# Two of four weight sums formed by adding transfers instead of VectorE in the seven-product pairs of a decoder layer

## The chip, the cores and the metric

The kernel runs on one core of a Trainium2 chip. Its time is the device time of one execution in microseconds (us). Tensors stand in SBUF as 128 partitions by so many columns. TensorE (PE in the profile, PEld for its weight loads) multiplies, VectorE (DVE), ScalarE (ACT) and GpSimd (POOL) work element by element, and SyncE (SP) issues transfers between HBM and SBUF. POOL and ACT can issue transfers too.

## The reference

One decoder layer for 512 tokens of width 1024 in float32:

```python
h = rms_norm(x, ffn1_pre_g);  x = x + 0.5 * rms_norm(swiglu(h, ffn1_w_in, ffn1_w_out), ffn1_post_g)
h = rms_norm(x, mix_pre_g);   proj = h @ w_mix_in          # attention and a state space model
...
h = rms_norm(x, ffn2_pre_g);  x = x + 0.5 * rms_norm(swiglu(h, ffn2_w_in, ffn2_w_out), ffn2_post_g)

def swiglu(x, w_in, w_out):
    gate, up = jnp.split(x @ w_in, 2, axis=-1)             # w_in: 1024 x 5632
    return (jax.nn.silu(gate) * up) @ w_out                # w_out: 2816 x 1024
```

The change touches `x @ w_in` of the two feed-forward layers.

## The kernel before

Every float32 product is formed from two halves of its operands: `hi` (rounded by ScalarE, `whi`) and `lo` (the rest, `wlo = raw - hi`, by VectorE or POOL), and three matmuls hi·hi, hi·lo, lo·hi. Making `whi` and `wlo` of a weight tile is called a split (line 107 for `wlo`, 105 for `whi`); `cut` does it for a pair's tile, and there are four `whi`/`wlo` buffers, so a split of one product's weights waits for PE to have finished the product four before.

The 2816 hidden units are 22 blocks of 128. The first 8 (first layer) or 6 (second layer) are computed directly. The others come in pairs of blocks, f and f+1, by a scheme of Strassen's kind: the weights of a pair are a 2 x 2 array of tiles of 128 x 1024 floats (512 KB), a11 and a12 for the gate (first and second half of the inner dimension), a21 and a22 for the up projection. Seven products instead of eight need four sums of tiles: c3 = a11 + a21, c2 = c3 + a22, c1 = a21 + a22, and at last c2 + a12. On PE the products of a pair stand in this order, 24 matmuls of 256 columns each: `wx` with a11, `wy` with a12, `wx` with c2, `wq` with c1, `wx` with c3, `wq` with c2 + a12, `wx` with a22. In the chain of the profile two neighbouring `wx` products show as one piece of 48: a22 of one pair and a11 of the next. There are 7 pairs in the first layer (f = 8 to 20) and 8 in the second (f = 6 to 20); `outp`, the second matrix product (`yo`), stands between groups of them.

The function `seven` makes two closures: `sums` prepares sums and differences of the activations ahead of the pairs (n1, n2, t3, t4, in buffers `wsum`), and `pair` does one pair. a11 and a12 are loaded into buffers `wraw` (three, shared by all weights), a21 and a22 into `wx` (three), and all loads are issued by SP, in one order. VectorE forms the sums into `wsum` (three buffers) and makes `wlo`, except for a12 and a22, whose `wlo` is made by POOL (`cut(..., True)`). A scheduler sets the order on each engine by its own costs; only instructions marked `fix` keep the written order. Each engine works through its own list in order, so an instruction that waits holds up those behind it.

Of the kernel before, what the change touches and what calls it, by code (L numbers as in the profile page):

```python
# [8 lines left out]
F32 = mybir.dt.float32  # L9
# [3 lines left out]
ALU = mybir.AluOpType  # L13
# [4 lines left out]
P = 128  # L18
S = 512
# [3 lines left out]
NF = FF // P  # L23
# [3 lines left out]
QOFF = (0, 128, 384, 768, 1280)  # L27
RING = 8
NSTD = (8, 6)
PLACES = [(f"tq{q}{i}", 1) for q in range(3) for i in range(2)] + 3 * [("wsum", 3)]  # L30
BLOCKS = (2, 3, 0, 1)
HT = S // 2
H = 8
# [10 lines left out]
class Layer:  # L44
# [449 lines left out]
    def seven(self, fin, w_in, ig, r, ah, al):  # L494

        nc, V = self.nc, self.nc.vector
        more = [fin]  # L500
        wsum = lambda: more[0].tile([P, 1024], F32, name="wsum", tag="wsum", bufs=3)
        wx = lambda: fin.tile([P, 1024], F32, name="wx", tag="wx", bufs=3)
        gp = lambda: fin.tile([P, 1024], F32, name="gp", tag="gp", bufs=2)
        tq = []
        v4 = lambda t: t.rearrange("p (k c) -> p k c", c=HT)
        blocks = []

        def sums(early=False):

            q = [[gp(), gp()], [wx(), wx()]]  # L510

            def scaled(i):
                for j in range(2):
                    c = slice(j * HT, (j + 1) * HT)
                    for k in range(4):
                        V.scalar_tensor_tensor(out=v4(q[i][j])[:, k], in0=self.x(4 * i + k)[:, c],
                                               scalar=self.g(ig, 4 * i + k), in1=r[:, c], op0=ALU.mult, op1=ALU.mult)
                return q[i]

            b11, b12 = scaled(0)  # L520
            b21, b22 = scaled(1)
            more[0] = (yield) or fin
            tq.extend([more[0].tile([P, 1024], F32R, name="tq", tag=f"tq{i}{j}") for j in range(2)] for i in range(3))
            n1, n2, t4 = wsum(), wsum(), wsum()
            V.tensor_tensor(out=n1, in0=b11, in1=b12, op=ALU.subtract)
            yield
            bh, bl = [self.b16(n, F32R) for n in ("bh", "bl")] if early else (None, None)
            v = lambda t, i: t.rearrange("p (q k) c -> p q (k c)", q=4)[:, i]

            def plain(*ts):  # L530
                for t in ts:
                    i = len(blocks)
                    blocks.append((v(bh, i), v(bl, i)))
                    self.split(*blocks[i], t)

            if early:
                plain(b11)
            V.scalar_tensor_tensor(out=n2, in0=n1, scalar=-1.0, in1=b22, op0=ALU.mult, op1=ALU.subtract)
            if early:
                plain(b21)  # L540
            yield
            V.scalar_tensor_tensor(out=t4, in0=n2, scalar=-1.0, in1=b21, op0=ALU.mult, op1=ALU.subtract)
            self.split(*tq[0], n2)
            t3 = wsum()
            V.tensor_tensor(out=t3, in0=b22, in1=b12, op=ALU.subtract)
            yield
            if early:
                plain(b22, n1)
            yield
            self.split(*tq[1], t3)  # L550
            yield
            self.split(*tq[2], t4)
            if not early:
                yield
                bh, bl = [self.b16(n, F32R) for n in ("bh", "bl")]
                plain(b11, b21, b22, n1)
            yield

        def block(f, up, kh):
            t = wx() if up else self.wp.tile([P, 1024], F32, name="wraw", tag="wraw", bufs=3)  # L560
            src = w_in[f + NF * up:f + NF * up + 2, :, kh * S:(kh + 1) * S].rearrange("f p c -> p f c")
            nc.sync.dma_start(out=t.rearrange("p (f c) -> p f c", f=2), in_=src)
            return t

        def cut(t, pool=False):
            hi, lo = (self.wp.tile([P, 1024], F32R, name=n, tag=n, bufs=4) for n in ("whi", "wlo"))
            self.wsplit(t, hi, lo, pool)
            return hi, lo

        def times(bank, w, xb, first):  # L570
            for g in range(2):
                for k in range(4):
                    c, m = slice(k * HT, (k + 1) * HT), slice((4 * g + k) * P, (4 * g + k + 1) * P)
                    st = first and g == 0 and k == 0
                    for i, (wi, xi) in enumerate(((0, 0), (0, 1), (1, 0))):
                        self.mm(bank[:, g * HT:(g + 1) * HT], lhsT=w[wi][:, m], rhs=xb[xi][:, c],
                                start=st and i == 0, stop=g == 1 and k == 3 and i == 2, skip_group_check=True)

        def keep(bank):
            t = self.tmp("kp")  # L580
            nc.scalar.copy(out=t, in_=bank)
            return t

        def pair(f, late=False):
            (b11, b21, b22, n1), (n2, t3, t4) = blocks, tq
            add = lambda x, z, t: V.tensor_tensor(out=t, in0=x, in1=z, op=ALU.add)
            p2 = lambda t: t.rearrange("p (f c) -> p f c", f=2)
            half = lambda t, h: t[:, :, h * HT:(h + 1) * HT]
            gt = p2(gp())
            X = self.bank("wx")  # L590
            a11 = block(f, 0, 0)
            times(X, cut(a11), b11, True)
            s1 = keep(X)
            a12 = block(f, 0, 1)
            h12 = cut(a12, True)
            Y = self.bank("wy")
            times(Y, h12, b21, True)
            V.tensor_tensor(out=half(gt, 0), in0=p2(Y), in1=p2(s1), op=ALU.add)
            a21, a22 = block(f, 1, 0), block(f, 1, 1)
            c3 = wsum()  # L600
            add(a11, a21, c3)
            c2 = wsum()
            add(c3, a22, c2)
            times(X, cut(c2), n2, False)
            s2 = keep(X)
            c1 = wsum()
            add(a21, a22, c1)
            Q = self.bank("wq")
            times(Q, cut(c1), n1, True)
            q = keep(Q)  # L610
            times(X, cut(c3), t3, False)
            V.tensor_tensor(out=q, in0=X, in1=q, op=ALU.add)
            add(c2, a12, c2)
            times(Q, cut(c2), b22, False)
            V.tensor_tensor(out=half(gt, 1), in0=p2(Q), in1=p2(s2), op=ALU.add)
            nc.scalar.activation(out=gt, in_=gt, func=AF.Silu)
            times(X, cut(a22, True), t4, False)
            s = f % RING
            dst = lambda t, h: half(t.pair(slice(s, s + 2)), h)
            for h, u in ((1, q), (0, X)):  # L620
                V.scalar_tensor_tensor(out=half(gt, h), in0=p2(u), scalar=-1.0, in1=half(gt, h), op0=ALU.mult, op1=ALU.mult)
                if late:
                    self.split(dst(ah, h), dst(al, h), half(gt, h))
            if not late:
                self.split(ah.pair(slice(s, s + 2)), al.pair(slice(s, s + 2)), gt)

        return sums, pair
# [84 lines left out]
    def finish(self, fin, y, tail):  # L712


        nc, V, fx = self.nc, self.nc.vector, self.fix
        xt = [self.wp.tile([P, 1024], F32, name="xt", tag="wraw", bufs=3) for b in range(3)]
        xt.append(fin.tile([P, 1024], F32, name="xt", tag="wx", bufs=3))
        for b in range(4):
            self.dma(out=xt[b], in_=self.xd[b].rearrange("p d c -> p (d c)"))
        xtt = lambda b, d: xt[b][:, d * S:(d + 1) * S]  # L720
# [17 lines left out]
        def at(t, b, i):  # L738
            d, sl = cols(*parts(b)[i])
            return t(b, d)[:, sl]  # L740
# [7 lines left out]
        def gain(b, i):  # L748
            d, sl = cols(*parts(b)[i])
            yg[b, i] = fin.tile([P, S], F32, name="yg", tag=PLACES[len(yg)][0],  # L750
                                bufs=PLACES[len(yg)][1])[:, :parts(b)[i][1]]
            fx(V.tensor_tensor(out=yg[b, i], in0=at(y, b, i), in1=self.gt[:, d, sl], op=ALU.mult))
# [29 lines left out]
        p, b = BLOCKS[-2:]  # L782
# [697 lines left out]
```

## Time and profile before

| what | us |
|---|---|
| median of 3 runs | 930.64 (930.52 to 931.39) |
| profiled execution | 929.2 |
| its span, first to last instruction | 927.4 |
| PE busy | 914.6 |
| VectorE busy | 650.2 |
| ScalarE busy | 442.6 |
| POOL busy | 213.7 |

In the profile, "L107 DVE ... wlo<-wsum,whi x60 | 73.3, 1221" is a group of 60 instructions of line 107 on VectorE that write wlo and read wsum and whi, 73.3 us in all and 1221 ns each. "<-" with an engine behind a time names what ended the engine's idle time. The start times of a timeline are us from the span's start; a matmul's duration overlaps the next one's start.

### The profile page before, as it was taken

How to read it: one execution, taken by the hardware profiler on the slowest of the kernel's cores; microseconds unless marked ns; L12 is line 12 of the kernel's file. 1: busy time of each engine (PE TensorE's matmuls, PEld its weight loads, DVE VectorE, ACT ScalarE, POOL GpSimd, SP SyncE). 2: the span in 40 equal slices, each digit the busy share in tenths (PEclk: the TensorE clock that was granted, in tenths of full speed). 3: DMA queues.
4: the chain of work that ended last, by engine and by line, in shares of the span. 5: the costliest groups of instructions: out<-in, count | busy, mean ns of one | idle time of the engine just before them, and what ended most of it. 6: DMA issues, size and time to landing. Idle time of an engine off the chain costs nothing.

```text
span 927.4 us, 15348 instructions
## 1 busy us (share of the span) xinstructions
PE 914.6 (99%) x6162; PEld 817.6 (88%) x6162; DVE 650.2 (70%) x1071; ACT 442.6 (48%) x685; POOL 213.7 (23%) x127
## 2 busy tenths in 40 slices
PE   9999999999999999999999999999999999999996
PEld 7887789998999989978777899888899989998995
DVE  6999694755577566758898568698367556755856
ACT  7263764552355443525745654482355414541542
POOL 0433202222223134500000025432122312231321
PEclk9999999999999999999999999999999999999999
DMA  8224652324231162283321440345223322332322
GB/s 274 91 69 139 213 207 90 110 84 132 84 117 44 58 195 90 88 207 122 114 69 56 162 148 24 84 167 182 92 93 113 114 92 94 112 114 93 94 88 90
DMA packets 47590, 106.81 MB, mean 115 GB/s; under 512 B 7808, under 2 KB 11136, under 8 KB 46976
## 3 DMA queue, kind: packets, MB, share of 16 engines
q1 hardware_dynamic: 45936, 102.21, 34.0%
q10 hardware_dynamic: 1584, 3.63, 1.1%
q8 instruction: 48, 0.79, 0.3%
q14 instruction: 22, 0.18, 0.1%
HBM read 96.13 MB, written 9.70 MB: 114 GB/s over the span
## 4 chain that ended last, share of the span: by engine, by line
PE 82%; DVE 3%; DMA 2%; issue 1%; ACT 1%; POOLq 0%; POOL 0%; DVEq 0%; SPq 0%; ACTq 0%
PE yo L132 21%; PE wx L132 18%; PE wq L132 9%; PE yt L132 6%; PE gu L132 5%; PE first L132 5%; PE wy L132 5%; PE prj L132 4%; PE prv L132 2%; PE mo L132 2%; PE st L132 1%; PE ys L132 1%; DMA w1d<-w1s 1%; PE pt L1070 1%; PE sc L132 1%
## 5 line engine op out<-in xcount | busy, mean ns | idle before, releaser
L105 ACT CAST whi<-wraw 128x1024 fp32r<-128x1024 f32 (+5 forms) x129 | 125.1, 977 | 164.3 <-PE yo L132 65.5
L107 POOL TENSOR_TENSOR wlo<-wraw,whi 128x1024 fp32r<-128x1024 f32 (+1 forms) x41 | 109.3, 2665 | 305.0 <-ACT whi L105 297.7
L107 DVE TENSOR_TENSOR wlo<-wraw,whi 128x1024 fp32r<-128x1024 f32 (+5 forms) x88 | 106.9, 1222 | 87.6 <-ACT whi L105 87.4
L132 PE MATMUL wx<-tq,whi 128*128 128x256 f32 x720 | 129.3, 280 | 0.0
L132 PEld LDWEIGHTS wx<-tq,whi 128*128 128x128 f32 x720 | 110.3, 188 | 0.0
L107 DVE TENSOR_TENSOR wlo<-wsum,whi 128x1024 fp32r<-128x1024 f32 x60 | 73.3, 1221 | 46.7 <-ACT whi L105 46.7
L105 ACT CAST whi<-wsum 128x1024 fp32r<-128x1024 f32 x60 | 62.9, 1049 | 90.2 <-PE yo L132 28.0
L132 PE MATMUL wx<-tq,wlo 128*128 128x256 f32 x360 | 100.4, 279 | 0.0
L107 POOL TENSOR_TENSOR wlo<-wx,whi 128x1024 fp32r<-128x1024 f32 x15 | 39.1, 2608 | 185.1 <-ACT whi L105 185.1
L132 PE MATMUL gu<-xh,wlo 128*128 128x512 f32 x176 | 69.0, 392 | 1.9 <-POOL wlo L107 1.2
L132 PE MATMUL gu<-xh,whi 128*128 128x512 f32 x176 | 70.6, 401 | 0.0
L132 PE MATMUL gu<-xl,whi 128*128 128x512 f32 x176 | 68.6, 390 | 0.0
L132 PE MATMUL wq<-bh,wlo 128*128 128x256 f32 x240 | 68.1, 284 | 0.0
L132 PE MATMUL wq<-bh,whi 128*128 128x256 f32 x240 | 68.0, 283 | 0.0
L132 PE MATMUL wq<-bl,whi 128*128 128x256 f32 x240 | 67.9, 283 | 0.0
L132 PEld LDWEIGHTS wx<-tq,wlo 128*128 128x128 f32 x360 | 67.6, 188 | 0.0
L132 PE MATMUL yo<-ah,whi 128*128 128x512 f32 x144 | 56.3, 391 | 0.0
L132 PE MATMUL yo<-whi,ah 128*128 128x512 f32 x144 | 56.1, 389 | 0.0
L132 PE MATMUL yo<-ah,wlo 128*128 128x512 f32 x144 | 56.1, 389 | 0.0
L132 PE MATMUL yo<-al,whi 128*128 128x512 f32 x144 | 56.0, 389 | 0.0
L132 PE MATMUL yo<-whi,al 128*128 128x512 f32 x144 | 56.0, 389 | 0.0
L132 PE MATMUL yo<-wlo,ah 128*128 128x512 f32 x144 | 56.0, 389 | 0.0
(261 smaller groups left out, 2384.8 us busy)
## 6 DMA issues: line engine op xcount, KB each, us to landing
wraw<-w1i SPq DMA_DIRECT2D x28, 512.0 KB, 3.6
wraw<-w2i SPq DMA_DIRECT2D x28, 512.0 KB, 3.6
wraw<-w2o SPq DMA_DIRECT2D x18, 512.0 KB, 3.8
wx<-w2i SPq DMA_DIRECT2D x16, 512.0 KB, 3.7
wx<-w1i SPq DMA_DIRECT2D x14, 512.0 KB, 3.6
wraw<-wmi SPq DMA_DIRECT2D x12, 512.0 KB, 3.8
wraw<-w1o SPq DMA_DIRECT2D x8, 512.0 KB, 4.3
wraw<-w1o SPq DMA_DIRECT2D x8, 384.0 KB, 3.0
```

Source lines behind the costliest of these rows:

```text
L105: fix(self.nc.scalar.copy(out=hi, in_=raw))
L107: fix(eng.tensor_tensor(out=lo, in0=raw, in1=hi.bitcast(F32), op=ALU.subtract))
L132: i = self.nc.tensor.matmul(*a, **k)
L1070: self.fix(nc.tensor.transpose(b[i][:, o:o + P], sc[:, c:c + P], self.ident))
```

## The change

c3 and c1 are no longer formed by VectorE. SP loads the first block (a11 for c3, a21 for c1) straight into a `wsum` buffer, and POOL then issues a second transfer that adds the other block to it on the way (`accum_op`). a11 and a22 are needed by themselves as well and are still loaded, so a pair has seven transfers of 512 KB, and a21 no longer has a tile of its own. The second transfer waits until the first has landed. The sums c2 and c2 + a12 stay on VectorE. `wsum` has four buffers instead of three and `wx` two instead of three.

```diff
-PLACES = [(f"tq{q}{i}", 1) for q in range(3) for i in range(2)] + 3 * [("wsum", 3)]
+PLACES = [(f"tq{q}{i}", 1) for q in range(3) for i in range(2)] + 3 * [("wsum", 4)]
...
-        wsum = lambda: more[0].tile([P, 1024], F32, name="wsum", tag="wsum", bufs=3)
-        wx = lambda: fin.tile([P, 1024], F32, name="wx", tag="wx", bufs=3)
+        wsum = lambda: more[0].tile([P, 1024], F32, name="wsum", tag="wsum", bufs=4)
+        wx = lambda: fin.tile([P, 1024], F32, name="wx", tag="wx", bufs=2)
...
+        def src(f, up, kh):
+            return w_in[f + NF * up:f + NF * up + 2, :, kh * S:(kh + 1) * S].rearrange("f p c -> p f c")
+
...
+        def both(x, z):
+            t = wsum()
+            v = t.rearrange("p (f c) -> p f c", f=2)
+            nc.sync.dma_start(out=v, in_=src(*x))
+            nc.gpsimd.dma_start(out=v, in_=src(*z), accum_op=ALU.add)
             return t
...
-            a21, a22 = block(f, 1, 0), block(f, 1, 1)
-            c3 = wsum()
-            add(a11, a21, c3)
+            c3 = both((f, 0, 0), (f, 1, 0))
+            a22 = block(f, 1, 1)
             c2 = wsum()
             add(c3, a22, c2)
...
-            c1 = wsum()
-            add(a21, a22, c1)
+            c1 = both((f, 1, 0), (f, 1, 1))
...
-        xt.append(fin.tile([P, 1024], F32, name="xt", tag="wx", bufs=3))
+        xt.append(fin.tile([P, 1024], F32, name="xt", tag="wx", bufs=2))
```

VectorE, first layer, while PE works on pair f=18. Before (wsum_2958 is c3 of f=18, wsum_2960 its c2 and then c2 + a12; wsum_3187, 3189 and 3221 are c3, c2 and c1 of f=20; wraw_3119 is a11 of f=20):

```order
L107 TENSOR_TENSOR wlo_3026<-wsum_2958,whi_3025 128x1024
L586 TENSOR_TENSOR wsum_3187<-wraw_3119,wx_3183 128x1024
L598 TENSOR_TENSOR gp_2888<-wy_2928,kp_2920 128x2x256
L107 TENSOR_TENSOR wlo_3056<-wsum_2960,whi_3055 128x1024
L586 TENSOR_TENSOR wsum_3189<-wsum_3187,wx_3185 128x1024
L586 TENSOR_TENSOR wsum_3221<-wx_3183,wx_3185 128x1024
L107 TENSOR_TENSOR wlo_3122<-wraw_3119,whi_3121 128x1024
```

After, at the same place (wsum_2954 is c3 of f=18, wsum_2959 its c2; wsum_3183 and 3188 are c3 and c2 of f=20, wx_3186 its a22):

```order
L107 TENSOR_TENSOR wlo_3026<-wsum_2954,whi_3025 128x1024
L597 TENSOR_TENSOR wsum_3188<-wsum_3183,wx_3186 128x1024
L609 TENSOR_TENSOR gp_2888<-wy_2928,kp_2920 128x2x256
L107 TENSOR_TENSOR wlo_3056<-wsum_2959,whi_3055 128x1024
L107 TENSOR_TENSOR wlo_3122<-wraw_3119,whi_3121 128x1024
```

The sums of c3 and c1 are gone, and the sum c2 of the next pair has moved up to where c3's stood, ahead of the split of c2 + a12.

POOL, first layer, pairs f=16 to f=20. Before (wx tiles are a22 of f=16, 18 and 20, wraw tiles a12 of f=18 and 20):

```order
L107 TENSOR_TENSOR wlo_2857<-wx_2727,whi_2856 128x1024
L107 TENSOR_TENSOR wlo_2925<-wraw_2922,whi_2924 128x1024
L107 TENSOR_TENSOR wlo_3086<-wx_2956,whi_3085 128x1024
L107 TENSOR_TENSOR wlo_3154<-wraw_3151,whi_3153 128x1024
L107 TENSOR_TENSOR wlo_3315<-wx_3185,whi_3314 128x1024
```

After (wsum_2991 is c1 of f=18, wsum_3183 and wsum_3220 are c3 and c1 of f=20):

```order
L573 DMA wsum_2991<-w1i 128x2x512
L107 TENSOR_TENSOR wlo_2857<-wx_2728,whi_2856 128x1024
L573 DMA wsum_3183<-w1i 128x2x512
L107 TENSOR_TENSOR wlo_2925<-wraw_2922,whi_2924 128x1024
L573 DMA wsum_3220<-w1i 128x2x512
L107 TENSOR_TENSOR wlo_3086<-wx_2957,whi_3085 128x1024
L107 TENSOR_TENSOR wlo_3154<-wraw_3151,whi_3153 128x1024
L107 TENSOR_TENSOR wlo_3315<-wx_3186,whi_3314 128x1024
```

An adding transfer now stands ahead of each split, for c1 of the next pair before a22 and for c3 of the pair after that before a12 (f=20 is the layer's last pair, so its two splits have none).

SP, the loads for f=18 and f=20. Before:

```order
L562 DMA wx_2954<-w1i 128x2x512
L562 DMA wx_2956<-w1i 128x2x512
L562 DMA wraw_2922<-w1i 128x2x512
L562 DMA wraw_3119<-w1i 128x2x512
L562 DMA wx_3183<-w1i 128x2x512
L562 DMA wx_3185<-w1i 128x2x512
L562 DMA wraw_3151<-w1i 128x2x512
```

After:

```order
L572 DMA wsum_2954<-w1i 128x2x512
L564 DMA wx_2957<-w1i 128x2x512
L564 DMA wraw_2922<-w1i 128x2x512
L564 DMA wraw_3119<-w1i 128x2x512
L572 DMA wsum_2991<-w1i 128x2x512
L572 DMA wsum_3183<-w1i 128x2x512
L564 DMA wx_3186<-w1i 128x2x512
L564 DMA wraw_3151<-w1i 128x2x512
```

The buffer of c1 of f=18 (wsum_2991) is the one that c3 of f=16 had, and that of c3 of f=20 (wsum_3183) the one that c2 of f=16 had; their loads wait on SP for the splits of those, and a22 of f=20 waits behind them.

More of the change, by code (lines that the diff above doesn't have):

```diff
@@ L557, in sums @@
             yield
+        def src(f, up, kh):
+            return w_in[f + NF * up:f + NF * up + 2, :, kh * S:(kh + 1) * S].rearrange("f p c -> p f c")
         def block(f, up, kh):
             t = wx() if up else self.wp.tile([P, 1024], F32, name="wraw", tag="wraw", bufs=3)
-            src = w_in[f + NF * up:f + NF * up + 2, :, kh * S:(kh + 1) * S].rearrange("f p c -> p f c")
-            nc.sync.dma_start(out=t.rearrange("p (f c) -> p f c", f=2), in_=src)
+            nc.sync.dma_start(out=t.rearrange("p (f c) -> p f c", f=2), in_=src(f, up, kh))
+            return t
+        def both(x, z):
[3 more added lines that the diff above has]
+            nc.gpsimd.dma_start(out=v, in_=src(*z), accum_op=ALU.add)
             return t
```

## The prediction

> **What bounds the kernel now.** I read four views in this order: the page's busy table and chain, the chain in order of time, the stage table, and the engines' timelines inside one pair. The page first:
>
> ```profile
> span 927.4 us, 15348 instructions
> PE   914.6 (99%) x6162; PEld 817.6 (88%) x6162; DVE 650.2 (70%) x1071; ACT 442.6 (48%) x685; POOL 213.7 (23%) x127
> PE 82%; DVE 3%; DMA 2%; issue 1%; ACT 1%; POOLq 0%; POOL 0%; DVEq 0%; SPq 0%; ACTq 0%
> ```
>
> The matmul engine PE is busy for all but 12.8 us of the span and carries the chain. A busy PE row is no proof by itself, so the chain inside the pairs comes next. These are pair f=16 from its last product on, then all of pair f=18 (from 282.37) and the start of f=20:
>
> ```profile
> 265.21 2.88 PE wy L132 x24
> ...
> 279.51 5.71 PE wx L132 x48
> 285.23 2.88 PE wy L132 x24
> 288.11 2.83 PE wx L132 x24
> 290.94 2.88 PE wq L132 x24
> 293.82 2.83 PE wx L132 x24
> 296.65 2.88 PE wq L132 x24
> 299.54 5.71 PE wx L132 x48
> ```
>
> Each product of 24 matmuls starts where the last one ends, about 0.12 us a matmul, and the same product returns 20.02 us later (wy at 265.21 and 285.23). Nothing but PE stands on the chain. The stage table says whether that holds for all pairs (columns: window, PE, PEld, DVE, ACT, POOL busy, granted clock, DMA share, GB/s):
>
> ```profile
> 149.60:209.60 60.00, 60.00 (x505) 60.00 (x505) 38.33 (x39) 31.00 (x36) 14.54 (x6) 1.00 0.28 92
> 242.30:322.30 80.00, 80.00 (x674) 80.00 (x673) 53.93 (x56) 40.62 (x47) 18.16 (x7) 1.00 0.23 74
> 673.00:733.00 60.00, 60.00 (x505) 60.00 (x505) 38.66 (x39) 31.71 (x37) 14.79 (x6) 1.00 0.29 99
> 765.70:825.70 60.00, 60.00 (x506) 60.00 (x505) 39.45 (x41) 31.21 (x35) 15.10 (x6) 1.00 0.30 100
> 858.40:898.40 40.00, 40.00 (x338) 40.00 (x337) 26.57 (x26) 21.74 (x25) 12.83 (x5) 1.00 0.27 85
> 242.30:262.30 20.00, 20.00 (x171) 20.00 (x170) 12.96 (x14) 9.64 (x12) 4.84 (x2) 1.00 0.32 106
> 282.40:302.40 20.00, 20.00 (x170) 20.00 (x169) 14.92 (x16) 10.70 (x13) 5.47 (x2) 1.00 0.10 27
> 545.00:612.00 67.00, 66.24 (x502) 62.56 (x501) 49.45 (x93) 30.99 (x60) 30.09 (x27) 1.00 0.30 95
> 898.40:927.40 29.00, 22.00 (x109) 18.49 (x107) 19.90 (x39) 7.13 (x20) 2.63 (x4) 0.96 0.25 97
> ```
>
> The first five rows are all fifteen pairs: 300 us, 20.0 each, and PE is busy for 300 of 300 at a granted clock of 1.00. VectorE (DVE) is busy about two thirds of that time. No pair waits for DVE. The two single pairs (rows six and seven) run at DMA shares of 0.32 and 0.10 and both take 20.0 us, so more transfer traffic did not slow PE there.
>
> **The change, part by part.**
>
> *Removed: two VectorE sums a pair.*
>
> ```profile
> L586 DVE TENSOR_TENSOR wsum<-wraw,wx 128x1024 f32<-128x1024 f32 x15 | 18.3, 1222 | 9.2 <-DMA wraw<-w2i 8.6 <-DMA wraw<-w1i 0.5
> L586 DVE TENSOR_TENSOR wsum<-wx 128x1024 f32<-128x1024 f32 x15 | 18.3, 1219 | 0.2
> ```
>
> 15 x (1.222 + 1.219) = 36.6 us of VectorE work go. On the path: 0, since PE has no idle time in the pairs to give back.
>
> *Added on the queues.* A pair issued 4 transfers of 512 KB, all on SP. It now issues 5 plain ones on SP (the two first blocks go into the sum buffers, and a11 and a22 still come by themselves) and 2 accumulating ones on POOL. These are three more a pair, 45 x 0.524 MB = 23.6 MB in all. The prices:
>
> ```profile
> wraw<-w1i SPq DMA_DIRECT2D x28, 512.0 KB, 3.6
> um<-ud SPq DMA_DIRECT2D x4, 256.0 KB, 7.9
> DMA to landing us min/median/max: 3.5/3.6/6.6
> 276.14 0.37 SPq L562 DMA_DIRECT2D wraw<-w1i  x1
> ```
>
> The third row is the summary for tile wx: a 512 KB load lands 3.5 to 6.6 us after its issue. One SP issue costs 0.37 us, 0.37 x 1 more a pair, beside 20 us of PE. Of the sixteen transfer engines, 0.28 x 60 us moved 92 GB/s x 60 us = 5.5 MB, so a 512 KB transfer takes 1.6 us of all of them. The pair asks for 5 x 1.6 + 2 x (1.6 to 3.2) = 11.2 to 14.4 of its 20 us, where 3.2 prices an add as two transfers. That fits.
>
> The trace has no transfer issued by POOL and no accumulating one. Two prices are unknown: d, the time POOL spends on issuing one, and T, from that issue to the landing. For d the ends are 0.37 us (SP's issue of the same shape) and 6.82 us (the longest pass of POOL over such a tile, in the timeline below); I take 1.5, nearer to SP's, because an issue names 2 x 128 rows and does not pass over 131,072 elements. For T the ends are 3.5 us (the fastest plain landing) and 7.9 us (the slowest median landing in the quoted rows); I take 5, in the middle of the wx rows.
>
> *Where d and T lie.* Timelines of pair f=16 and the start of f=18, then the longest POOL pass:
>
> ```profile
> 266.38 1.22 DVE L107 TENSOR_TENSOR wlo<-wsum,whi 128x1024 fp32r<-128x1024 f32 x1
> 267.51 1.22 DVE L586 TENSOR_TENSOR wsum<-wraw,wx 128x1024 f32<-128x1024 f32 x1
> 269.25 1.21 DVE L107 TENSOR_TENSOR wlo<-wsum,whi 128x1024 fp32r<-128x1024 f32 x1
> 271.52 1.22 DVE L586 TENSOR_TENSOR wsum<-wx 128x1024 f32<-128x1024 f32 x1
> 272.02 3.01 POOL L107 TENSOR_TENSOR wlo<-wx,whi 128x1024 fp32r<-128x1024 f32 x1 [11.96 <-ACT whi L105]
> 277.68 2.41 POOL L107 TENSOR_TENSOR wlo<-wraw,whi 128x1024 fp32r<-128x1024 f32 x1 [2.65 <-ACT whi L105]
> 282.32 1.05 ACT L105 CAST whi<-wsum 128x1024 fp32r<-128x1024 f32 x1 [0.83 <-PE wx L132]
> 284.04 1.22 DVE L107 TENSOR_TENSOR wlo<-wsum,whi 128x1024 fp32r<-128x1024 f32 x1
> 287.57 1.22 DVE L586 TENSOR_TENSOR wsum<-wraw,wx 128x1024 f32<-128x1024 f32 x1
> 621.39 6.82 POOL L107 TENSOR_TENSOR wlo<-wraw,whi 128x1024 fp32r<-128x1024 f32 x1 [11.74 <-ACT whi L105]
> ```
>
> With four sum buffers, c1 of pair f=18 may be loaded once c3 of f=16 is split, at 266.38 + 1.22 = 267.6. SP issues, and the load lands at 267.7 + 3.6 = 271.3. POOL then issues the adding transfer, and behind it on POOL stands the split of a22 (before: 272.02). It runs from 271.3 + d for 3.01 us to 274.3 + d; with d = 1.5 that is 275.8, and its product starts at 279.51 (the first half of the x48 piece). Then POOL issues the add into c3 of f=20, whose load could start when c2 was split at 270.46 and so landed by 274.2. POOL is free at 274.3 + 2d = 277.3, before the split of a12 gets its input (277.68). So the splits are late by 0.8 us and by nothing, with slacks of 3.7 and 5.1 us left before PE asks (279.51, 285.23). Cost on the path: 0.
>
> The sums: c1 of f=18 is complete at 271.3 + T = 276.3, and its cast ran at 282.32, so T may be 11.0 without any effect. The cast's split ended at 285.26, 5.7 us before the product at 290.94. c3 of f=20 is complete at 275.8 + 5 = 280.8; the sum c2 that reads it takes the place at 287.57. Both ends of T fit.
>
> *The first pair* is the tightest place, since its buffers come free late:
>
> ```profile
> 132.87 2.35 DVE L152 TENSOR_TENSOR tq<-wsum,tq 128x1024 fp32r<-128x1024 f32 x2
> 139.69 2.44 POOL L107 TENSOR_TENSOR wlo<-wraw,whi 128x1024 fp32r<-128x1024 f32 x1 [30.57 <-ACT whi L105]
> 149.44 1.05 ACT L105 CAST whi<-wsum 128x1024 fp32r<-128x1024 f32 x1 [3.90 <-issue]
> ```
>
> c1's buffer holds t4 until 135.22; the load lands about 140, and on POOL the add stands behind the split of a12, to 142.13. With T = 5 it is there at 147.1, before its cast at 149.44; with 7.9 it is 0.6 late, against a product that starts 8.7 us after the cast. Cost 0.
>
> *Fourth sum buffer, third wx buffer gone.* t3 no longer waits for a buffer in the sums ahead of the pairs, where PE idles 67.00 - 66.24 = 0.8 us (window 545 to 612): between -0.8 and 0, taken as 0, as that idling is spread over matmuls that read no sum. a22 two pairs on waits for the split of a22 on POOL (275.8), lands by 280 and is read at 287.57: hidden.
>
> **The sum.** 0 on the path in all parts, against the profiled execution's 929.2 us (span 927.4 and 1.8 around it); the median of the runs is 930.6, 1.4 above it. Forecast: 930.6.
>
> **Rivals.**
>
> *POOL's order becomes the loop (slower).* From the end of the pair's first product (265.21) to the start of the next pair's second (285.23) now runs: split of c3 to 267.6 (2.4), load (3.7), d, split of a22 (3.01), d, split of a12 (2.41) = 11.5 + 2d, against 20.0. It decides from d = 4.25 on. Eight of the pair-to-pair steps carry both adds, so the time is 930.6 + 8 x (2d - 8.5): 942.6 at d = 5, 971 at d = 6.82. For it: POOL's pass took 3.01 us where the VectorE sum at 271.52 ran beside it, 2.41 where none did, and 6.82 at 621.39; if issuing stretches by the same 2.8 times, 1.5 becomes 4.2, at the edge. Against it: the sum at 271.52 is one of those removed. The Trainium skill, "SBUF — State Buffer", section "Who interferes with whom", says that a VectorE instruction with two SBUF inputs contends with POOL instructions that read SBUF and not with those that only write, and that writing transfer descriptors needs the write side (which it calls inferred). By that rule the passes stretch, as the rows show, and d does not, and the time stays 930.6; no row here shows an issue from POOL. Chance 0.12.
>
> *The adding transfers eat the transfer engines (slower).* They saturate when one add takes (20 - 5 x 1.6) / 2 = 6.0 us of all sixteen engines, 3.75 times a plain transfer. At 7 us, fifteen pairs are 2 us longer each: 960. Short of that, T over 11 starts to use up the 5.7 us of slack, so 932 to 940. For it: no row prices an add. Against: at a plain price the engines are under 0.6 busy. The Trainium skill, "Collectives: The Full Stack", section "The bandwidth ceiling: the fold count and why AG ≠ RS ≠ AR", says a reducing transfer reads two sources and so runs at half the rate of a copy; as an estimate that is 3.2 us an add and 14.4 of 20, short of saturation and of no effect on the time. No run here shows it yet. Chance 0.07.
>
> *VectorE relief pays after all (faster).* Only the tail has idle PE that VectorE follows (29.00 against 22.00 at the end). If the last pair's two sums, 2.4 us, had pushed work there: 928.2. Against: PE is busy for 40.00 of 40.00 up to 898.40, and the tail's work starts after. Chance 0.05.
>
> **How the numbers follow.** No change: 0.76, own range 929.2 to 932.2. A measurement of this kernel can tell about 0.2%, 1.9 us, from no change: faster 0.05, same 0.76, slower 0.19. The range reaches from 928.0, which takes in the tail case, to 936, which takes in the mild half of the late-transfer case; outside lie POOL's loop beyond d = 4.6 and saturation, together some 0.15.
>
> **What would show it.** Right: PE 60.00 of 60.00 in the pair stages; VectorE 36.6 us less; POOL with 30 issues of under 4 us; HBM reads up by 23.6 MB; the a22 split starting by about 273, the a12 split where it was. Wrong: gaps of PE at wy products, where a12 is split on POOL (d too long); gaps at c1 or c2 products with POOL idle (T too long); or a matmul step longer than 0.12 us at a DMA share above 0.32, which no row excludes.

## The result, and the profile after

The changed kernel takes 941.93 us (median of 4 runs, 940.29 to 946.38) against 930.58 of the kernel before (4 runs, 930.48 to 931.39): a ratio of 1.0128, with a 95% interval of 1.0091 to 1.0164. It is 11.3 us slower; the forecast was 930.6, no change. The profiled execution took 940.88. The times of kernels here and below are medians of their executions; one execution of delay_small, at 4347.42 us, is left out of its median. These are the lines of its page that answer to those shown of before, with the memory line:

```profile
span 939.1 us, 15444 instructions
PE   916.8 (98%) x6162; PEld 817.8 (87%) x6162; DVE 650.5 (69%) x1041; ACT 442.6 (47%) x685; POOL 243.1 (26%) x157
HBM read 119.72 MB, written 9.70 MB: 138 GB/s over the span
PE 74%; DVE 6%; issue 4%; DMA 3%; ACT 3%; POOL 1%; POOLq 0%; SPq 0%; DVEq 0%; ACTq 0%
```

VectorE has 30 instructions less (1041 against 1071) and is as busy as before: 650.5 us against 650.2. So the 36.6 us of sums are gone, and something of the same size has come in their place. PE carries 74% of the chain, where it carried 82%; VectorE, ScalarE, POOL and idle issue time have entered it. The stage table, in the columns of the prediction (window, PE, PEld, DVE, ACT, POOL, clock, DMA share, GB/s), shows where. Rows one to three are stages of three pairs each, all of which had PE busy throughout before; row four is the last two pairs of the second layer, where next to nothing is lost:

```profile
149.60:217.00 67.40, 64.80 (x523) 63.49 (x522) 48.08 (x37) 31.77 (x37) 24.49 (x14) 1.00 0.68 171
680.00:741.30 61.30, 60.33 (x506) 60.13 (x505) 42.58 (x35) 31.58 (x36) 21.31 (x12) 1.00 0.64 172
774.00:836.50 62.50, 60.58 (x505) 60.17 (x504) 44.26 (x37) 30.98 (x35) 21.58 (x12) 1.00 0.64 169
869.10:909.40 40.30, 40.27 (x338) 40.06 (x337) 25.55 (x24) 21.73 (x25) 14.20 (x6) 1.00 0.40 110
```

In the first three PE now idles 1.0 to 2.6 us. Its waits (what waited, for what; us in total, times, longest) name the releasers:

```profile
PE wx L132 <- ACT kp L592: 4.6, 5, 1.2
PE wx L132 <- POOL wlo L107: 0.8, 1, 0.8
PE yo L132 <- DVE al L152: 0.8, 1, 0.8
PE wy L132 <- POOL wlo L107: 0.6, 1, 0.6
```

PE's matmuls come in nearly the same order in both kernels, so the start of the same matmul in both traces can be subtracted. This difference grows in steps, and each step is a loss:

```
start before (us)   the product that starts late                 step (us)
166.84              a22 product, first pair (waits for POOL)     +1.07
172.56              a12 product, second pair (waits for POOL)    +0.85
195.22              c2 product                                   +1.41
214.95, 215.18      outp, waits for VectorE's al                 +1.59
287.94              c2 product                                   +0.91
515 to 523          the mix stage between the layers             +1.14
718.60              c2 product                                   +1.22
791.31              c2 product                                   +1.47
811.33              c2 product                                   +0.95
875.44              c2 product                                   +0.30
```

They sum to 10.9 of the 11.7 us of span. Six of the ten are c2 products, 6.3 us in all; the first two and the outp step make 3.5. The mix stage has no part of the change, and kernels below that issue no transfer on POOL lose as much there against the same trace of before (delay_2 1.1, delay_small 1.3 us): its step can't be put down to the change. The profiled execution of before lay 1.4 us under its median.

What happens at a c2 product is read from the engines' timelines. First the kernel before, pairs f=18 and f=20:

```profile
286.11 0.58 ACT L581 COPY kp<-wx 128x512 f32<-128x512 f32 x1
297.70 2.41 POOL L107 TENSOR_TENSOR wlo<-wraw,whi 128x1024 fp32r<-128x1024 f32 x1 [2.60 <-ACT whi L105]
300.58 1.23 DVE L107 TENSOR_TENSOR wlo<-wsum,whi 128x1024 fp32r<-128x1024 f32 x1 [0.31 <-ACT whi L105]
```

POOL's split of a12 ends at 300.11, and 0.47 us later VectorE starts its split of c2 of pair f=20, whose product is still 7 us away. Behind that split stand the pieces on VectorE that finish pair f=18, and behind those, on ScalarE, the copy of a psum bank (kp) that the same c2 product waits for. The first line is that copy one pair earlier: it ends at 286.69, 1.3 us ahead of the c2 product of f=18, which goes on adding into that bank (287.94 in the table). The same place in the changed kernel, pair f=18, 4.92 us later on the clock than before:

```profile
277.87 1.22 POOL L573 DMA_DIRECT2D wsum<-w1i  x1 [11.18 <-ACT kp L592]
278.66 2.87 POOL L107 TENSOR_TENSOR wlo<-wx,whi 128x1024 fp32r<-128x1024 f32 x1
284.06 1.21 POOL L573 DMA_DIRECT2D wsum<-w1i  x1 [2.53 <-DVE kp L621]
284.84 2.88 POOL L107 TENSOR_TENSOR wlo<-wraw,whi 128x1024 fp32r<-128x1024 f32 x1
285.61 3.20 DVE L107 TENSOR_TENSOR wlo<-wsum,whi 128x1024 fp32r<-128x1024 f32 x1 [0.27 <-ACT whi L105]
291.24 1.05 ACT L151 CAST ah<-gp 128x1024 fp32r<-128x1024 f32 x1 [2.79 <-DVE gp L630]
292.19 1.04 ACT L105 CAST whi<-wsum 128x1024 fp32r<-128x1024 f32 x1
293.14 0.57 ACT L592 COPY kp<-wx 128x512 f32<-128x512 f32 x1
293.77 0.51 PE L132 MATMUL wx<-tq,whi 128*128 128x256 f32 x2 [0.57 <-ACT kp L592]
```

POOL's second adding transfer goes out 6.19 us after the first, though POOL stands idle for 2.53 us ahead of it. The split of a12 behind it starts at 284.84 - 4.92 = 279.92 on the clock of before, where it started at 277.68. VectorE's split of c2 starts 0.77 us into that pass, and takes 3.20 us in place of 1.23: it ends 1.1 us after the pass does. From there the delay goes on in order: VectorE's gp, ScalarE's cast of ah, which now idles 2.79 us for it, the cast of the sum, the copy of the psum bank, and the c2 product, which finds the bank not yet copied. VectorE's split is 1.97 us longer, 1.3 of it were slack, and 0.7 are left over; the record shows 0.57 of waiting and the table a step of 0.91. The outp step has a like cause ahead of it: two splits of 128x768 on VectorE take 3.91 and 3.77 us beside passes of POOL, 0.96 each before.

Over the whole program this is what became of VectorE's saving: the mean of its splits of sums in ns, before and after.

```profile
L107 DVE TENSOR_TENSOR wlo<-wsum,whi 128x1024 fp32r<-128x1024 f32 x60 | 73.3, 1221 | 46.7 <-ACT whi L105 46.7
L107 DVE TENSOR_TENSOR wlo<-wraw,whi 128x1024 fp32r<-128x1024 f32 (+5 forms) x88 | 106.9, 1222 | 87.6 <-ACT whi L105 87.4
```

```profile
L107 DVE TENSOR_TENSOR wlo<-wsum,whi 128x1024 fp32r<-128x1024 f32 x60 | 90.1, 1502 | 43.9 <-ACT whi L105 43.9
L107 DVE TENSOR_TENSOR wlo<-wraw,whi 128x1024 fp32r<-128x1024 f32 (+5 forms) x88 | 133.3, 1522 | 113.1 <-ACT whi L105 113.0
```

16.8 + 26.4 = 43.2 us more for the same 148 splits. Less the 36.6 us removed, and less 6.3 us by which the sum c2 got shorter (15 x (1.637 - 1.220), its mean before and after), that is the +0.3 of the page, to within what overlaps and smaller rows make (some 1 us).

### The profile page after: what moved, and what is told of

It is laid out like the page before. It is cut to its first block, busy times and chain, and to the rows that moved or that the text cites. A ratio compares the mean times of both kernels' runs of the same rounds, so it can differ in the third digit from the quotient of the medians.

```text
span 939.1 us, 15444 instructions
## 1 busy us (share of the span) xinstructions
PE 916.8 (98%) x6162; PEld 817.8 (87%) x6162; DVE 650.5 (69%) x1041; ACT 442.6 (47%) x685; POOL 243.1 (26%) x157
## 3 DMA queue, kind: packets, MB, share of 16 engines
q0 software_dynamic: 8160, 15.73, 10.3%
## 4 chain that ended last, share of the span: by engine, by line
PE 74%; DVE 6%; issue 4%; DMA 3%; ACT 3%; POOL 1%; POOLq 0%; SPq 0%; DVEq 0%; ACTq 0%
PE yo L132 20%; PE wx L132 14%; PE wq L132 9%; PE yt L132 6%; PE gu L132 5%; PE first L132 5%; PE prj L132 4%; PE wy L132 3%; PE prv L132 2%; DVE wlo L107 1%; ACT whi L105 1%; PE st L132 1%; PE mo L132 1%; DMA w1d<-w1s 1%; PE ys L132 1%
## 5 line engine op out<-in xcount | busy, mean ns | idle before, releaser
L107 DVE TENSOR_TENSOR wlo<-wraw,whi 128x1024 fp32r<-128x1024 f32 (+5 forms) x88 | 133.3, 1522 | 113.1 <-ACT whi L105 113.0
L107 DVE TENSOR_TENSOR wlo<-wsum,whi 128x1024 fp32r<-128x1024 f32 x60 | 90.1, 1502 | 43.9 <-ACT whi L105 43.9
L573 POOL DMA_DIRECT2D wsum<-w2i x16 | 19.5, 1220 | 124.7 <-DMA wsum<-w2i 56.2
```

The costliest lines, as they stand in the source:

```text
L107: fix(eng.tensor_tensor(out=lo, in0=raw, in1=hi.bitcast(F32), op=ALU.subtract))
L573: nc.gpsimd.dma_start(out=v, in_=src(*z), accum_op=ALU.add)
```

## The experiments

Three theories were set against each other. *Collision*: a pass of POOL over a weight block makes VectorE's two-input instructions stand still, and the change moves the a12 pass onto one of them. *Traffic*: the transfer engines, busy 0.64 to 0.68 of the pair stages after 0.28, make loads late. *Price*: each adding transfer, or the wait for its landing, costs something by itself. Within the first it was open why the second adding transfer goes out so late. Each ratio below is to executions of the kernel before that ran beside that kernel, with medians of 930.3 to 930.6.

### The collision without any transfer

The kernel before, with one-input copies ahead of the a12 split on POOL, which are overwritten by it:

```
             nc.scalar.copy(out=hi, in_=t)
             eng = nc.gpsimd if pool else V
+            for _ in range(n):                  # delay_big 1, delay_2 2, delay_3 3
+                eng.tensor_copy(out=lo, in_=hi) # delay_small: one copy of 256 columns
             eng.tensor_tensor(out=lo, in0=t, in1=hi.bitcast(F32), op=ALU.subtract)
```

What was expected of delay_small, delay_big, delay_2 and delay_3, in this order:

> The kernel before, all sums on VectorE and no transfer on POOL, with a copy of 256 of the 1024 columns put on POOL ahead of the split of a12, so that the split starts a little later. Theory A (a POOL pass that covers VectorE's split of c2 is what costs): the pass ended 0.47 us ahead of that split, so a delay of about 0.4 us costs nothing: 930 to 932. Theory B (transfers): 930 to 931.

> The kernel before, no transfer on POOL, with a copy of all 1024 columns on POOL ahead of the split of a12: the split starts and ends 1 to 2 us later, across VectorE's split of c2. Theory A: that split takes 2.5 to 4 us in place of 1.23 and the product of c2 waits about 1 us in most pairs; 936 to 944, without a single transfer more than before. Theory B (transfers, or the wait for landing): 930 to 931.

> The kernel before with two copies of 1024 columns on POOL ahead of the split of a12: 1.1 us each by the run with one copy, so the split starts 2.2 us later and ends about 1.7 us after VectorE's split of c2 has started. One copy (ended 0.64 us after that start) cost 0.5 us of that split and no time. Theory A (collision): the split now takes 2.7 to 3.2 us, the slack of the psum copy behind it on ScalarE is used up, PE waits some tenths to 1 us a pair; 933 to 941. Theory B (transfers): 930 to 931.

> The same with three copies, 3.3 us: the pass now starts ahead of VectorE's split of c2 by about 0.4 us or less, or just after it. Theory A: if it still starts first, that split takes up to 3.5-3.9 us and the time is 938 to 947; if VectorE gets in first, the pass waits instead and VectorE's next pieces are held. Theory B: 930 to 931.

```
               delay of the a12 split   time (us)   ratio   95% interval
delay_small    0.48 us                  931.02      1.0010  1.0001 to 1.0020
delay_big      1.1                      930.91      1.0008  0.9999 to 1.0016
delay_2        2.2                      935.58      1.0054  1.0041 to 1.0067
delay_3        3.3                      944.05      1.0143  1.0130 to 1.0156
```

One copy was expected to lose 6 to 14 us and lost nothing: it stretched VectorE's split only to 1.72 us, inside the 1.3 us of slack of the psum copy. Two copies lose what the collision theory says, with not one transfer added, and their splits of sums average 1502 ns, as in the changed kernel. Three copies lose 13.4 us; a time was named only for the case that POOL starts first, and VectorE did. POOL and VectorE of delay_2, then of delay_3, with PE's wait in each:

```profile
302.13 2.40 POOL L571 TENSOR_TENSOR wlo<-wraw,whi 128x1024 fp32r<-128x1024 f32 x1
302.80 2.82 DVE L571 TENSOR_TENSOR wlo<-wsum,whi 128x1024 fp32r<-128x1024 f32 x1 [0.31 <-ACT whi L567]
PE wx L132 <- ACT kp L585: 2.7, 10, 0.6
```

```profile
306.15 1.44 DVE L571 TENSOR_TENSOR wlo<-wsum,whi 128x1024 fp32r<-128x1024 f32 x1 [0.31 <-ACT whi L567]
306.59 3.26 POOL L571 TENSOR_TENSOR wlo<-wraw,whi 128x1024 fp32r<-128x1024 f32 x1
307.51 2.90 DVE L625 SCALAR_TENSOR_TENSOR gp<-kp,gp 128x512 f32<-128x512 f32 x1
PE wx L132 <- ACT kp L585: 10.9, 10, 1.4
```

In delay_2 POOL is first and VectorE's split waits, 2.82 us. In delay_3 VectorE is first by 0.44 us: its split takes 1.44, POOL's pass is stretched from 2.41 to 3.26, and VectorE's next two-input instruction, 0.69 us long elsewhere, takes 2.90. The wait of PE is the one of the changed kernel, wx for ACT's kp. The Trainium skill, "SBUF — State Buffer", section "Who interferes with whom", says that a VectorE instruction with two SBUF inputs contends with a POOL instruction that reads SBUF, and that the order of issue decides who blocks; both traces agree. In the changed kernel, gp<-wq,kp, one of whose inputs is a psum bank, keeps its 0.69 us inside a pass (at 166.88). There the order can't be read off the recorded starts: behind an adding issue, splits of VectorE that start 0.11 and 0.63 us ahead of POOL's pass wait all the same (4.08 us at 881.61, 3.77 at 211.03).

### Why the second adding transfer is late

The program sets the size of a scratch for the descriptors of POOL's transfers (the records by which a transfer is handed over); it is doubled. The kernel before has the same 1024, with no transfer on POOL to use it.

```
-    nc = bacc.Bacc(..., dynamic_dma_scratch_size=1024)
+    nc = bacc.Bacc(..., dynamic_dma_scratch_size=2048)
```

> The scratch for descriptors of POOL's transfers is doubled, 1024 to 2048; nothing else. Theory A1 (the second adding transfer of a pair waits 6.1 us because the descriptors of the first still fill the scratch): the two issues come within about 2 us of each other, the a12 split goes back to about 1 us or less behind its old place, the mean of VectorE's splits falls to about 1.25-1.3 us and the time to 930 to 935. Theory A2 (it waits for its own first block, which lands late because it shares the transfer engines with the adding transfer): spacing stays 6.1 us and the time 940 to 943.

932.67 us, ratio 1.0030 (1.0016 to 1.0045): 9.3 of the 11.3 us come back. POOL's timeline of the same pair f=18 (1.5 us later on the clock than before), and the split group:

```profile
273.41 1.22 POOL L573 DMA_DIRECT2D wsum<-w1i  x1 [11.77 <-DMA wsum<-w1i]
274.19 2.89 POOL L107 TENSOR_TENSOR wlo<-wx,whi 128x1024 fp32r<-128x1024 f32 x1
276.57 1.69 POOL L573 DMA_DIRECT2D wsum<-w1i  x1
279.28 2.39 POOL L107 TENSOR_TENSOR wlo<-wraw,whi 128x1024 fp32r<-128x1024 f32 x1 [1.02 <-ACT whi L105]
L107 DVE TENSOR_TENSOR wlo<-wsum,whi 128x1024 fp32r<-128x1024 f32 x60 | 76.1, 1269 | 43.3 <-ACT whi L105 43.3
```

The second transfer goes out 3.16 us after the first, while the split between them still runs, and the a12 split waits for its input from ScalarE again: 279.28 - 1.48 = 277.80, where before had 277.68. VectorE is busy 616.2 us, 34.0 less than before. Nothing but the scratch differs, so the wait is one for room in it: with 1024 the second transfer goes out when the first has landed. The traces bear this out pair by pair, with the same lag however long the landing takes:

```
                             first lands after   second goes out after its issue (us)
changed kernel, f=18         5.88                6.19
changed kernel, at 650.07    7.72                8.04
a22dve (below), at 280.46    9.99                10.31
doubled scratch, f=18        6.52                3.16
```

In all thirteen places of the changed kernel where two transfers follow each other so, the lag behind the landing is 0.26 to 0.32 us. The releaser that the trace names for the 2.53 us (DVE kp) is not the cause; no row names this resource. The buffers, the order and the bytes of the change are all still there with the doubled scratch, so they don't make these 9.3 us by themselves.

### What adding costs

```
-            nc.gpsimd.dma_start(out=v, in_=src(*z), accum_op=ALU.add)
+            nc.gpsimd.dma_start(out=v, in_=src(*z))
```

> POOL's transfers overwrite instead of adding, so the sums c1 and c3 leave out their first block; the first block is still loaded. If adding itself is dear (reading the target as well): issue to landing falls from 6.1 to about 4 us, the second issue of a pair comes 2 us sooner, the a12 split ends before VectorE's split of c2 starts and the time is 931 to 936. If what matters is that POOL issues at all and waits for the first block: landing stays 5.5 to 6.1 us, time 939 to 943.

930.99 us, ratio 1.0007 (0.9999 to 1.0016), with the scratch at 1024. The transfer rows (KB each, median us to landing) and the queue's share of the span, of the changed kernel and of this one, and two of its issues:

```profile
wsum<-w2i POOLq DMA_DIRECT2D x16, 512.0 KB, 6.0
wsum<-w1i POOLq DMA_DIRECT2D x14, 512.0 KB, 6.1
q0 software_dynamic: 8160, 15.73, 10.3%
```

```profile
wsum<-w2i POOLq DMA_DIRECT2D x16, 512.0 KB, 5.2
wsum<-w1i POOLq DMA_DIRECT2D x14, 512.0 KB, 4.9
q0 software_dynamic: 4320, 15.73, 5.0%
273.15 0.73 POOL L573 DMA_DIRECT2D wsum<-w1i  x1 [11.83 <-ACT whi L105]
276.28 0.72 POOL L573 DMA_DIRECT2D wsum<-w1i  x1
```

For the same 15.73 MB, adding takes 8160 packets in place of 4320, and 10.3% of 939.1 us / 30 = 3.2 us of all sixteen engines a transfer in place of 5.0% of 929.8 / 30 = 1.55. Two overwriting transfers fit the small scratch together: the second goes out 3.13 us after the first, before that has landed. So the same number of bytes and of POOL transfers, without the added packets, costs nothing that can be told. Landing fell by 1 us, not by the 2 expected of dear adding, and yet the whole loss went: the gain is the second issue, which no longer waits for the first to land.

### Which pass of POOL

```
-            h12 = cut(a12, True)            # a12dve, nopool: on VectorE
+            h12 = cut(a12)
-            times(X, cut(a22, True), t4, False)  # a22dve, nopool: on VectorE
+            times(X, cut(a22), t4, False)
```

What was expected of a12dve, a22dve and nopool, in this order:

> The split of a12 moves from POOL to VectorE; transfers stay as in the changed kernel. Theory A (collision): VectorE's two-input splits stand still while POOL passes over a12, and that pass now comes so late that it covers the split of c2. Without it the mean of VectorE's splits of sums falls from 1502 ns to about 1.25-1.30 us (the a22 pass on POOL remains), PE's gaps before the product of c2 go, and the time is 930 to 935. Theory B (traffic): the transfer engines at 0.64 to 0.68 make loads land late or slow the memory; nothing about that is changed here, so 940 to 943.

> The changed kernel (scratch 1024) with the split of a22 on VectorE and the split of a12 left on POOL. If the late a12 pass across VectorE's split of c2 is what costs: the second adding transfer still waits for the first, the a12 pass stays late, and the time stays 938 to 942.5. If either pass of POOL costs about as much: 935 to 938. If the a22 pass is the one: 931 to 933.

> Both splits of POOL in a pair, a12 and a22, move to VectorE; POOL keeps only the adding transfers. Theory A: no POOL pass beside any split in the pairs, so every VectorE split takes 1.22 us; VectorE gets 30 x 1.22 = 36.6 us of new work in place of the two sums that were taken away, and the time is 929.5 to 932.5, also because the adding transfer of the first pair no longer holds the a22 split. Theory B: same traffic, 940 to 943. If VectorE's order is what hurts (its work in order behind waits), slower than moving a12 alone.

a12dve 932.31 (ratio 1.0024, 1.0013 to 1.0035), a22dve 944.67 (1.0163, 1.0143 to 1.0182), nopool 933.22 (1.0036, 1.0022 to 1.0051). The first fell in its range; a22dve came out 2 us and nopool 0.7 us above theirs. The transfers are the same in all three, so traffic alone is out as the cause of the 11 us. The a12 pass does the harm; with a22 off POOL it comes later still, since there the first adding transfer of many pairs lands only about 8 to 10 us after its issue, and PE waits for the pass directly. PE's main wait in a22dve, and the one in the pairs of a12dve (first pair, the adding transfer that waits for its first block and holds the a22 split):

```profile
PE wy L132 <- POOL wlo L107: 8.3, 4, 4.4
```

```profile
PE wx L132 <- POOL wlo L107: 1.0, 1, 1.0
```

### One sum alone

c1only keeps the loaded and added c1 and makes c3 on VectorE, c3only the other way round. In their first form (c1only, c3only) they kept the four sum and two wx buffers of the change, so that a21 and a22 shared two; the forms with 33 in the name have three and three, as before.

```
-            c1 = both((f, 1, 0), (f, 1, 1))   # c3only
+            c1 = wsum()
+            add(a21, a22, c1)
-            c3 = both((f, 0, 0), (f, 1, 0))   # c1only
+            c3 = wsum()
+            add(a11, a21, c3)
```

What was expected of c1only, c3only, c1only_33 and c3only_33, in this order:

> Only c1 is made by a load and an adding transfer; c3 is a VectorE sum again (scratch 1024, four sum buffers). If the waiting of the second adding transfer for the first one's descriptors is the cause, one a pair never waits: the a12 split stands where it stood before the change, VectorE's splits of sums average 1.22 to 1.30 us, 930.5 to 932.5 (up to 1.3 us stay in the first pair, where the adding transfer waits for its first block and holds the a22 split). If each adding transfer has its price, half of the loss: 935 to 937.

> Only c3 is made by a load and an adding transfer; c1 is a VectorE sum again. If the waiting of the second for the first is the cause: 930 to 932, the adding transfer issued as soon as its first block has landed. If each adding transfer has its price, half of the loss: 935 to 937.

> Only c1 by an adding transfer, with three sum buffers and three wx buffers as in the kernel before (the run with four and two had a21 and a22 share two wx buffers). If the waiting of the second adding transfer for the first one's descriptors is the cause of the loss: 930.5 to 933. If each adding transfer has its own price: 935 to 937. If the buffers were not what made the run with two wx buffers slow: 945 or more.

> Only c3 by an adding transfer, with three sum buffers and three wx buffers. If the waiting of the second for the first is the cause: 930.5 to 933; with only three sum buffers the first block of c3 is loaded later than in the changed kernel, which can hold the a12 split on POOL behind the adding transfer: up to 940 then. If each adding transfer has its own price: 935 to 937. If the buffers were not what made the run with two wx buffers slow: 970 or more.

c1only 948.5 (ratio 1.0195) and c3only 981.47 (1.0547), neither as expected. The likely reason, as the next two runs changed both numbers of buffers at once: two wx buffers do not feed a pair that loads a21 and a22 into them. With three and three, c1only_33 takes 931.42 (1.0006, 0.9997 to 1.0014): one adding transfer a pair has no price. c3only_33 takes 961.15 (1.0326, 1.0301 to 1.0351), beyond what was expected. Its VectorE, and PE's wait:

```profile
280.86 1.23 DVE L597 TENSOR_TENSOR wsum<-wsum,wx 128x1024 f32<-128x1024 f32 x1 [5.99 <-DMA wsum<-w1i]
PE wx L132 <- DVE kp L622: 20.2, 7, 3.2
```

With three sum buffers c3's first block is loaded so late that VectorE stands 5.99 us for the adding transfer's landing, and all behind it on VectorE with it; there are 13 such waits, 66 us in all. That is the wait for landing which the price theory meant. The changed kernel has two, 10.9 us, both in the first pairs of the first layer; that the fourth sum buffer keeps the others away is likely, but no run has the changed kernel with three.

### The last two us

```
-            times(X, cut(a22, True), t4, False)     # ring_a22: scratch 2048
+            times(X, cut(a22, f != 8), t4, False)
```

nopool_ring is nopool with the scratch of 2048, and ring_a22_b is ring_a22 profiled a second time. What was expected of ring_a22, nopool_ring and ring_a22_b, in this order:

> The doubled scratch (2048), and in pairs f=8 the split of a22 on VectorE in place of POOL. With the doubled scratch alone 932.7 was measured, and PE lost 1.2 us in one place, the c2 product of the second pair (f=10 of the first layer), behind a first pair in which the adding transfer into c1 waits for its own first block and holds the a22 split and then the a12 split on POOL. If that hold is the rest of the loss: the gap goes, 930.5 to 931.7. If the rest is spread (more traffic, waits for landing): 932 to 933.5.

> Both splits of POOL in a pair on VectorE and the doubled scratch: no POOL pass and no wait for descriptors in the pairs, all 30 adding transfers kept. The four versions with 30 adding transfers and no long collision stand 1.9 to 3.0 us above the kernel before, the one with 30 overwriting transfers 0.5. If the rest was waits for descriptors and leftovers of the collision: 930.5 to 931.5. If it belongs to the adding transfers themselves (landing late from run to run): again 932 to 934.

> The kernel with doubled scratch and the a22 split of f=8 on VectorE once more, for a second profile: its first profiled run took 931.4, while the others ran from 931.3 to 936.1. If this one falls at 933 or more, the place where PE waits in it shows what the rest is: a first block or an adding transfer that lands late (theory of the transfers), or the first pair again.

ring_a22 took 933.42 (1.0033, 1.0020 to 1.0046), no better than the doubled scratch alone, though the step at the c2 product of the second pair shrank from 1.2 to 0.5 us in its profiled run; its runs spread from 931.3 to 936.1, and the second profile fell at 931.3, so it shows nothing of the slower ones. nopool_ring took 931.22, ratio 1.0005 (0.9997 to 1.0014). Its pair stage of the first layer:

```profile
149.60:209.60 60.00, 60.00 (x504) 59.84 (x503) 40.42 (x41) 30.95 (x36) 9.12 (x7) 1.00 0.75 186
```

PE is busy for 60.00 of 60.00 us with the transfer engines at 0.75. With neither POOL passes nor a wait for descriptors, all 30 adding transfers cost nothing that can be told. Without the passes but with that wait (nopool, 2.8 us) the loss goes through a landing: PE waits for ScalarE's kp at the c2 product of the second pair, and ScalarE had waited for an adding transfer that landed 8.28 us after its issue, with POOL idle:

```profile
172.49 1.05 ACT L105 CAST whi<-wsum 128x1024 fp32r<-128x1024 f32 x1 [4.54 <-DMA wsum<-w1i]
PE wx L132 <- ACT kp L592: 1.4, 1, 1.4
```

So a late landing can cost too. Where the longer executions of ring and ring_a22 (up to 938.83 and 936.14) lose their time stays open. No version was faster than the kernel before.

## Why the prediction was wrong

- **PE bounds the pairs, so VectorE's relief is worth 0.** Right, where the relief was had: with the doubled scratch VectorE does 34.0 us less, and the time does not fall below that of before.
- **d, POOL's time for one issue: taken 1.5.** Measured 1.22; the rival of a loop on POOL from d = 4.25 did not come. (Its 971 at d = 6.82 is 971.7 by its own sum.)
- **T: taken 5, up to 7.9, hidden.** The medians are 6.0 and 6.1 (5.7 to 7.8; with the doubled scratch, where two are out at once, 7.0 and 7.8), and T is hidden from PE: no wait of PE in the pairs names a landing. What it does hold is the issue of the next adding transfer, which the sum had no term for. With three sum buffers T is not hidden (c3only_33).
- **The adding transfers fit the transfer engines.** Right. The price of 3.2 us an add as two transfers, the upper end, is what was measured (3.2), and the trace agrees with the Trainium skill's rule in "Collectives: The Full Stack", section "The bandwidth ceiling: the fold count and why AG ≠ RS ≠ AR", half the rate of a copy: 3.2 against 1.55. Reads rose by 23.6 MB, as worked out. At a share of 0.75 PE lost nothing.
- **The step that failed first:** "POOL is free at 274.3 + 2d = 277.3, before the split of a12 gets its input (277.68)", so late "by nothing". It let the second adding transfer go out as soon as POOL was free, at 275.8. It went out at 284.06 - 4.92 = 279.14, since the first one held the descriptor scratch until it had landed: a wait that the sum put at nothing, though the size of the scratch stands in the program. With the doubled scratch it went out at 276.57 - 1.48 = 275.09 and the a12 split at 277.80: the step is right to 0.7 us when that wait is gone.
- **The step that failed next, and cost the time:** the slack of POOL's splits was counted to PE's demand alone (3.7 and 5.1 us). A split 2.2 us late is early enough for PE. The slack that decided was the 0.47 us to VectorE's next split, and behind that the 1.3 us of the kp copy before the c2 product. delay_2, late by the same 2.2 us, loses 5 us, delay_3 13.4.
- **The rule was at hand and used on one side only.** The prediction quoted the contention of VectorE and POOL for what it does to POOL's passes and to d. Its other side, VectorE standing still for the rest of a pass, was not priced; its splits got 43.2 us longer, more than the 36.6 us saved. The trace of before had a sign of it, the mean of 1.637 of the c2 sum against 1.22 of its siblings. Three of the fifteen, all in the second layer, took 3.30 us beside a pass of POOL; the group, and one of them:

```profile
L586 DVE TENSOR_TENSOR wsum<-wsum,wx 128x1024 f32<-128x1024 f32 x15 | 24.6, 1637 | 0.3
832.45 2.79 POOL L107 TENSOR_TENSOR wlo<-wraw,whi 128x1024 fp32r<-128x1024 f32 x1 [8.96 <-ACT whi L105]
833.02 3.30 DVE L586 TENSOR_TENSOR wsum<-wsum,wx 128x1024 f32<-128x1024 f32 x1
```

- **The first pair, cost 0.** Wrong by 1.9 us. The first block of the first c1, taken to land about 140, let its adding transfer go out at 145.16, and the one behind it, held by the scratch, at 151.28; so the second pair's buffers come free late, its adding transfer into c1 (164.21) waits for its own first block and holds the splits of a22 and a12, and PE waits for POOL at both (1.07 and 0.85). With the doubled scratch neither step is there: the wait for descriptors has its part in these too.
- **Gaps of PE at wy or at c2 with POOL idle** were named as signs of too long a d or T. The gaps at c2 did come with POOL idle (from 287.72 to 299.75 around the one at 293.77), but not for T: the pass that caused them had ended 5 us earlier. The sign as it was put would have led to the wrong term.

## What to carry to other kernels

Where two engines block each other, as POOL and VectorE here, the slack of an instruction ends where the other engine's next two-input instruction starts, not where its result is needed: before work is moved or queued ahead on POOL, lay its passes beside VectorE's in time, and add only the slack that stands behind that instruction (1.3 us here). When transfers go onto POOL's queue, count the descriptors that are out at once against the scratch, an adding transfer nearly twice by the packets of this case (8160 against 4320), and leave room for all of them. Busy time taken off an engine that isn't the bound buys nothing, but a shift of 2 us beside it can cost 1%.

## What the runs showed of the hardware that was not expected

- VectorE's instructions with both inputs in SBUF don't slow down by a share beside a two-input pass of POOL (2.4 to 2.9 us): they wait for it to end (1.22 to 3.20, 0.69 to 2.90 us). The 128x1024 splits of the changed kernel that start well inside a pass all end 1.1 us after it. If VectorE is first, POOL's pass waits (2.41 to 3.26 in delay_3).
- An adding issue on POOL without a pass does not hold VectorE: in nopool, splits that run beside one take 1.21 to 1.23 us.
- An adding transfer of 512 KB takes 1.22 us of POOL to issue, an overwriting one 0.72; 3.2 against 1.55 us of the sixteen engines; 6.0 to 6.1 against 4.9 to 5.2 us to landing (medians of the changed kernel and of the overwriting one).
- A descriptor scratch of 1024 kept a second adding transfer back until 0.26 to 0.32 us after the first had landed, 6.0 to 8.0 us after its issue in the changed kernel; at 2048 it followed after 3.16, behind the start of the split that stands between them. No view of the profile names that wait.
